# Keeping the split weights of the first half of the tokens in DRAM for the second half

## The chip, the core and the metric

The kernel runs on one core of a Trainium2 chip. The metric is device microseconds from the start to the end of one execution. Five engines work side by side, each through its own list of instructions, strictly in the order of that list: TensorE (PE; its weight loads are listed as PEld), VectorE (DVE), ScalarE (ACT), GpSimd (POOL) and SyncE (SP). They wait for each other through semaphores. DMAs are issued by SP and POOL here and carried out by 16 DMA engines.

## The reference, cut to what matters

One decoder layer, for 1024 prompt tokens and 8 decode tokens, all in float32:

```
h    = rmsnorm(x) ; proj = h @ w_in                # w_in: 1024 x 2304 = 18 tiles of 128 columns
pool = pooling mixer of proj[:, :512]              # tiles 0 to 3
rwkv = RWKV-7 mixer of proj[:, 512:]               # tiles 4 to 17, a recurrence over the tokens
x    = x + concat(pool, rwkv) @ w_out
x    = x + relu(rmsnorm(x) @ w_up)^2 @ w_down ; y = rmsnorm(x)
```

## The kernel before, in words

A float32 product is made of three fast ones. A weight `W` is split into `h` (W rounded to the format that TensorE takes at full rate, float32r) and `l = W - h`; the tokens likewise. `gemm` (L177) adds up h·h, h·l and l·h. So each weight costs, beside its load, one rounding copy on ACT and one subtraction on DVE.

`weights(src)` (L155) does this in pieces of 128 x 512 (256 KB): POOL loads the piece into a buffer `wr` (4 of them), ACT writes `wh`, DVE writes `wl` (6 buffers each). One column tile of `w_in` is two pieces. A piece can be split only when TensorE has finished with the piece six before it.

The input projection goes twice through all 18 tiles of `w_in`, because the tokens go in two halves: `project` (L272) and `pool_group` (L731) are called with `half` 0 and 1, and each time call `weights` for the tile. For a tile, TensorE does two token blocks of 24 matmuls of 256 columns, written into `pj`. Tiles are taken in the order 16, 17 (low rank inputs, `z`), 8, 4, 12 (k, r, v of the first head pair), 9, 5, 13, then the pool tiles 0 to 3, then 10, 6, 14, 11, 7, 15. A string, `ORDER` (L40), names the steps; within it a scheduler puts every instruction into its engine's list when the kernel is built, by its own estimate of when the inputs are there. So a change in one place can move instructions on every engine.

Around the projections, `stage1` (L346) prepares the recurrence for a head pair (it ends in `bv`, the matmul `pb`, and the matmuls `sc` and `bkt`), `inverse` (L474) inverts small triangular blocks through DRAM, and `chain` (L569) runs the recurrence (`pcs`, `py`) with short dependent steps on TensorE, ACT and DVE, whose result `ys` POOL stores to a scratch tensor `mix`. TensorE fills the time between chain steps with projections. `later_tokens` (L818) brings in the tokens of the second half; their raw tiles `xr` use the `wr` buffers too. The output projection (`mx`) and the MLP (`up`, `dn`) follow.

Of the kernel before, what the change touches and what calls it, by code (L numbers as in the profile page):

```python
# [8 lines left out]
F32R = mybir.dt.float32r  # L9
# [6 lines left out]
P = 128  # L16
D = 1024
# [19 lines left out]
NWH = 6  # L37
# [50 lines left out]
def build(nc, tc, I, O, dbg=None):  # L88
    with ExitStack() as ctx:
        _build(ctx, nc, tc, I, O, dbg or {})  # L90


def _build(ctx, nc, tc, I, O, dbg):
    V, A, PE, SY, GP = nc.vector, nc.scalar, nc.tensor, nc.sync, nc.gpsimd

    def f32(ap):
        return ap.bitcast(F32)

    def act(out, in_, func=AF.Copy, bias=0.0, scale=1.0, **k):
        A.activation(out, in_, func, bias=bias, scale=scale, **k)  # L100

    def open_pool(stack, name, bufs=1, **k):
        return stack.enter_context(tc.tile_pool(name=name, bufs=bufs, **k))
# [6 lines left out]
    wp = open_pool(ctx, "weights")  # L110
    ps_d = open_pool(ctx, "psd", 2, space=PSUM)
    ps_m = open_pool(ctx, "psm", 2, space=PSUM)
    dr = open_pool(ctx, "scratch", space=DRAM)
# [38 lines left out]
        act(out, out, AF.Exp, scale=-1.0, bias=last_bias)  # L152


    def weights(src, into=None):  # L155

        out = []
        n = int(np.prod(src.shape[1:]))
        for o in range(0, n, 512):
            w = min(512, n - o)  # L160
            raw = wp.tile([P, 512], F32, tag="wr", name="wr", bufs=NWR)
            if len(src.shape) > 2:
                GP.dma_start(raw.rearrange("p (m c) -> p m c", c=P), src)
            else:
                GP.dma_start(raw[:, :w], src[:, o:o + w])
            if into:
                h, l = into
            else:
                h = wp.tile([P, 512], F32R, tag="wh", name="wh", bufs=NWH)
                l = wp.tile([P, 512], F32R, tag="wl", name="wl", bufs=NWH)  # L170
            with tc.high_priority(offset=LEADW):
                act(h[:, :w], raw[:, :w])
                V.tensor_tensor(l[:, :w], raw[:, :w], f32(h[:, :w]), op=ALU.subtract)  # L173
            out += [(h[:, c:c + P], l[:, c:c + P]) for c in range(0, w, P)]
        return out

    def gemm(ps, w, ops):  # L177
# [84 lines left out]
    def project_block(m, w, b, use):  # L262
        n = SEG[b][1]
        first = m == 17 and b < 2
        ps = (ps_y if first else ps_d).tile([P, 512], F32, tag="y" if first else "d", name=f"pj{m}_{b}")
        gemm(ps[:, :n], w, [(X[b][0][:, k, :n], X[b][1][:, k, :n]) for k in range(KT)])
        with tc.high_priority(offset=LEADE):
            use(b, n, ps, X[b][2])

    ahead, late = {}, {}  # L270

    def project(m, half, use):  # L272
        w = ahead.pop(m, None) or weights(I["w_in"][m])
        for b in (2 * half, 2 * half + 1):
            if b in late:
                with tc.high_priority(offset=LEADX):
                    next(late.pop(b))
            project_block(m, w, b, use)
# [6 lines left out]
    def shifted(j, half, out):  # L285

        mu = col(V_MU, j)

        def use(b, n, ps, rs):
            l0 = 256 * (b % 2)  # L290
            pr = s1.tile([P, 264], F32, tag="pr", name=f"pr{j}_{b}", bufs=3)
            V.tensor_tensor(pr[:, :n], ps[:, :n], rs[:, :n], op=ALU.mult)
            act(out[:, l0:l0 + n], pr[:, :n], scale=omu[:, j:j + 1])
            d = out[:, l0 + 1:l0 + 256]
            V.scalar_tensor_tensor(d, pr[:, 0:255], mu, d, ALU.mult, ALU.add)
            if b:
                d = out[:, l0:l0 + 1]
                V.scalar_tensor_tensor(d, carry[:, j:j + 1], mu, d, ALU.mult, ALU.add)
            if b < 3:
                act(carry[:, j:j + 1], pr[:, 255:256])  # L300
            else:
                d = out[:, l0 + 256:l0 + 264]
                V.scalar_tensor_tensor(d, prevT[:, j, :], mu, d, ALU.mult, ALU.add)
                act(tailS[:, j, :], pr[:, 255:264])

        project(4 + j, half, use)
# [424 lines left out]
    def pool_group(g, half):  # L731
        win = 2 << g
        u, d = big(f"u{g}_{half}", f"u{g % 2}"), big(f"d{g}_{half}", f"d{g % 2}")
        e = d if g == 0 else big(f"e{g}_{half}", "e")
        if half:
            act(u[:, 0:16], ucar[:, g, :])
        else:
            GP.memset(u[:, 0:16], 0.0)

        def use(b, n, ps, rs):  # L740
            l0 = 16 + 256 * (b % 2)
            V.tensor_tensor(u[:, l0:l0 + n], ps[:, :n], rs[:, :n], op=ALU.mult)

        w = weights(I["w_in"][g])
        for i in range(2):
            project_block(g, w, 2 * half + i, use)
            yield
        n = HALF[half][1]
        pw_sb = pp.tile([P, P], F32, tag="pw", name=f"pw{g}_{half}")
        GP.dma_start(pw_sb, I["pool_w"][g])  # L750
        if half:
            act(tailU[:, g, :], u[:, 16 + 497:16 + 520])
        else:
            act(ucar[:, g, :], u[:, 512:528])
        src, w, i, o = u, 1, g % 2, 1
        while w < win:
            dst = (d, e)[i]
            V.tensor_tensor(dst[:, o:528], src[:, o:528], src[:, o - w:528 - w], op=ALU.add)
            src, w, i = dst, 2 * w, 1 - i
            o += w  # L760
        c = 16
        if half:
            V.tensor_tensor(poold[:, g, :], poold[:, g, :], u[:, 528:536], op=ALU.add)
            V.scalar_tensor_tensor(d[:, 528:536], poold[:, g, :], 1.0 / win, u[:, 528:536], ALU.mult, ALU.subtract)
        else:
            V.tensor_tensor(d[:, 16:32], d[:, 16:32], cst[:, C_RC + 16 * g:C_RC + 16 * g + 16], op=ALU.mult)
            V.tensor_tensor(d[:, 16:32], d[:, 16:32], u[:, 16:32], op=ALU.subtract)
            c = 32
        V.scalar_tensor_tensor(d[:, c:528], d[:, c:528], 1.0 / win, u[:, c:528], ALU.mult, ALU.subtract)
        yield  # L770
        for o, w in ((0, 256), (256, n - 256)):
            ps = ps_m.tile([P, 512], F32, tag="m", name=f"po{g}_{half}_{o}")
            PE.matmul(ps[:, :w], pw_sb, d[:, 16 + o:16 + o + w], start=True, stop=True)
            act(d[:, 16 + o:16 + o + w], ps[:, :w], scale=col(V_PS, g))
        QM.dma_start(mix_d[g][half], d[:, 16:16 + n])
# [3 lines left out]
    def pools(half, part):  # L779

        if part == 0:
            groups[half] = [pool_group(g, half) for g in range(4)]
        for g in ((0, 1, 0, 1, 0, 1), (2, 3, 2, 3, 0, 1, 2, 3), (2, 3))[part]:
            next(groups[half][g], None)
# [6 lines left out]
    units = [Unit(n % 4, n // 4) for n in range(8)]  # L791

    starts = [token_block(b) for b in range(2)]
    ahead[16] = weights(I["w_in"][16, :, 0:512])
    next(starts[0])
    ahead[16] += weights(I["w_in"][16, :, 512:])
    for t in starts:
        next(t)
    ahead[17] = weights(I["w_in"][17])
    SY.dma_start(cst, I["consts"])  # L800
    for t in starts:
        next(t)
# [15 lines left out]
    def later_tokens():  # L818
        with tc.high_priority(offset=LEADX):
            late.update((b, token_block(b)) for b in (2, 3))  # L820
            next(late[2])
            ahead[16] = weights(I["w_in"][16])
            next(late[3])

    st_d = ExitStack()
# [9 lines left out]
    for c in ORDER.split():  # L835
        if c[0] in calls:
            call, of = calls[c[0]]
            call(of[int(c[1])])
        elif c[0] == "P":
            pools(int(c[1]), int(c[2]))  # L840
        else:
            {"Q": pool_rows, "T": later_tokens, "L": lambda: low_rank(1), "D": decode_start}[c]()
# [14 lines left out]
    def x1s(m, c, n):  # L857

        h = int(c >= 512)
        return x1[h][:, m, c - 512 * h:c - 512 * h + n]  # L860
# [74 lines left out]
    with tc.tile_pool(name="opb", bufs=1, reuse_waits="tile") as op:  # L935
        ops = [mixed(op, k, 1, 3) for k in range(KT - 1)]
        for m in range(KT):
            w = weights(I["w_out"][m, :, :(KT - 1) * P])
# [12 lines left out]
    w = weights(I["w_up"][0])  # L951
# [20 lines left out]
    for g in range(7):  # L972
        ups_of(4 * g + 4)
        for m in range(KT):
            w = weights(I["w_down"][g, m])
# [20 lines left out]
    for b, (c, n) in enumerate(BLK):  # L996
        ss = ps_u.tile([P, 512], F32, tag="u", name=f"ss3{b}")
        acc = tmp(f"acc3{c}", "acc")[:, :n]
        for m in range(KT):
            down(7, m, b, ws[m])  # L1000
            d = x1s(m, c, n)
# [85 lines left out]
```

## Time and profile before

| | |
|---|---|
| median of 3 runs | 1378.54 us (1377.88 to 1382.42) |
| the profiled execution | 1379.3 us, its span 1377.5 us |
| TensorE busy | 1304.7 us, 95% of the span |
| VectorE busy | 809.3 us, 59% |
| ScalarE busy | 567.7 us, 41% |
| first half of the projection | about 9 to 194 us |
| second half | about 200 to 440 us |
| output projection and MLP | from about 470 us on |

The span runs from the first to the last instruction; the execution's own time is 1.8 us longer. From about 600 us on TensorE is never idle for long, and nothing there is touched by the change. A time written in brackets behind an instruction in the rows below is what its engine sat idle before it, and the arrow names what ended the wait.

### The profile page before, as it was taken

To read this page: it belongs to the slowest core of one execution; us is meant where nothing else is said; L and a number is where in the kernel's file an instruction comes from. 1 tells how busy PE (TensorE), PEld (TensorE's weight loads), DVE (VectorE), ACT (ScalarE), POOL (GpSimd) and SP (SyncE) were. 2 spreads that over 40 slices of the span, in tenths; PEclk is the share of its full clock that TensorE was granted. 3 is DMA by queue.
4 is the path that set the end of the run, shared out by engine and by line. 5 is a ranking of instruction groups with operands and counts; after the bars stand their busy time and mean duration, and the time that the engine had idled before them with its cause. 6 is when DMAs were issued, how large, how long until landed. Compare 5 with 4: busy or idle time off the path is not lost.

```text
span 1377.5 us, 24283 instructions
## 1 busy us (share of the span) xinstructions
PE 1304.7 (95%) x9748; PEld 1149.1 (83%) x9748; DVE 809.3 (59%) x1824; ACT 567.7 (41%) x1310; POOL 152.1 (11%) x301
## 2 busy tenths in 40 slices
PE   6999987999999899899999999999999999999996
PEld 6988776888877577699898999999999999999986
DVE  7887667748976754648644534435445354453447
ACT  7656775766766667626311211112112121121123
POOL 3112001101101100111000010100101000001000
PEclk9999997999999889989999999999999999999998
DMA  7234123311321542522111111111111111111103
GB/s 217 69 86 117 38 62 80 86 52 55 78 63 34 153 131 68 191 69 72 51 47 46 47 47 46 48 45 47 54 39 54 47 39 54 40 49 51 47 9 123
DMA packets 75312, 94.79 MB, mean 69 GB/s; under 512 B 46168, under 2 KB 52440, under 8 KB 75192
## 3 DMA queue, kind: packets, MB, share of 16 engines
q0 software_dynamic: 20480, 66.04, 15.4%
q1 hardware_dynamic: 53392, 25.36, 7.0%
q8 instruction: 76, 1.25, 0.4%
q10 hardware_dynamic: 1328, 1.85, 0.4%
q14 instruction: 36, 0.29, 0.1%
HBM read 79.67 MB, written 13.78 MB: 68 GB/s over the span
## 4 chain that ended last, share of the span: by engine, by line
PE 78%; ACT 9%; DVE 7%; issue 3%; DMA 3%; POOL 0%; SPq 0%; DVEq 0%; ACTq 0%; POOLq 0%
PE dn L183 26%; PE up L183 26%; PE pj L183 7%; PE mx L183 6%; PE sc L414 2%; ACT SV L100 1%; PE pcs L598 1%; PE pcs L592 1%; ACT Es L100 1%; DMA mr<-mix 1%; PE py L588 1%; ACT ys L100 1%; DVE wl L173 1%; DMA wr<-in_w_in 1%; DVE tm L515 1%
## 5 line engine op out<-in xcount | busy, mean ns | idle before, releaser
L100 ACT ACTIVATE wh<-wr 128x512 fp32r<-128x512 f32 x230 | 143.1, 626 | 359.6 <-PE dn L183 276.3
L183 PE MATMUL up<-h2h,wl 128*128 128x260 f32 (+1 forms) x768 | 245.6, 320 | 0.0
L183 PE MATMUL up<-h2h,wh 128*128 128x260 f32 (+1 forms) x768 | 245.0, 320 | 0.5 <-DVE u L929 0.5
L183 PE MATMUL up<-h2l,wh 128*128 128x260 f32 (+1 forms) x768 | 244.9, 319 | 0.0
L183 PE MATMUL dn<-uh,wl 128*128 128x512 f32 (+1 forms) x720 | 231.0, 321 | 0.0
L183 PE MATMUL dn<-ul,wh 128*128 128x512 f32 (+1 forms) x720 | 230.6, 320 | 0.0
L183 PE MATMUL dn<-uh,wh 128*128 128x512 f32 (+1 forms) x720 | 230.3, 320 | 0.0
L968 DVE TENSOR_TENSOR x<-dn,x 128x260 f32<-128x260 f32 (+1 forms) x192 | 99.0, 516 | 189.4 <-PE dn L183 189.4
L173 DVE TENSOR_TENSOR wl<-wr,wh 128x512 fp32r<-128x512 f32 x230 | 156.2, 683 | 55.3 <-ACT wh L100 51.9
L183 PE MATMUL pj<-xh,wh 128*128 128x256 f32 (+1 forms) x576 | 173.1, 301 | 12.6 <-ACT wh L100 9.5
L183 PE MATMUL pj<-xh,wl 128*128 128x256 f32 (+1 forms) x576 | 170.4, 296 | 0.0
L183 PE MATMUL pj<-xl,wh 128*128 128x256 f32 (+1 forms) x576 | 170.0, 295 | 0.0
L183 PEld LDWEIGHTS up<-h2l,wh 128*128 128x128 f32 x768 | 144.4, 188 | 12.2 <-DVE h2l L911 0.4
L183 PEld LDWEIGHTS up<-h2h,wh 128*128 128x128 f32 x768 | 144.2, 188 | 11.7 <-DVE u L929 0.9
L183 PEld LDWEIGHTS up<-h2h,wl 128*128 128x128 f32 x768 | 144.4, 188 | 11.1
L100 ACT ACTIVATE uh<-u 128x260 fp32r<-128x260 f32 (+1 forms) x96 | 47.2, 492 | 238.5 <-DVE u L930 238.5
L183 PEld LDWEIGHTS dn<-ul,wh 128*128 128x128 f32 x720 | 135.5, 188 | 10.9 <-issue 0.2
L183 PEld LDWEIGHTS dn<-uh,wh 128*128 128x128 f32 x720 | 135.7, 188 | 10.5
L183 PEld LDWEIGHTS dn<-uh,wl 128*128 128x128 f32 x720 | 135.4, 188 | 10.6 <-issue 0.2
L183 PEld LDWEIGHTS pj<-xh,wh 128*128 128x128 f32 x576 | 111.3, 193 | 18.3 <-ACT wh L100 9.5
L929 DVE SCALAR_TENSOR_TENSOR u<-up,rs 128x260 f32<-128x260 f32 (+1 forms) x96 | 49.5, 516 | 121.0 <-PE up L183 114.3
L183 PEld LDWEIGHTS pj<-xl,wh 128*128 128x128 f32 x576 | 111.3, 193 | 4.2 <-issue 3.3
(293 smaller groups left out, 2117.4 us busy)
## 6 DMA issues: line engine op xcount, KB each, us to landing
wr<-in_w_in POOLq DMA_DIRECT2D x72, 256.0 KB, 3.1
wr<-in_w_up POOLq DMA_DIRECT2D x64, 256.0 KB, 2.9
wr<-in_w_down POOLq DMA_DIRECT2D x64, 256.0 KB, 2.9
wr<-in_w_out POOLq DMA_DIRECT2D x26, 256.0 KB, 3.2
xr<-in_xT SPq DMA_DIRECT2D x16, 256.0 KB, 3.7
mr<-mix SPq DMA_DIRECT2D x8, 260.0 KB, 4.1
x<-in_xT SPq DMA_DIRECT2D x2, 1040.0 KB, 8.1
blk<-AA SPq DMA_DIRECT2D x16, 128.0 KB, 2.6
```

The lines of the kernel that those rows point to most:

```text
L100: A.activation(out, in_, func, bias=bias, scale=scale, **k)
L173: V.tensor_tensor(l[:, :w], raw[:, :w], f32(h[:, :w]), op=ALU.subtract)
L183: PE.matmul(ps, lhs, rhs, start=i == 0, stop=i == n - 1)
L414: PE.matmul(scs[h][:, c, :], BK[R[h], c, :, :], AR[R[h], c, :, h, :], start=True, stop=True)
L515: V.tensor_tensor(pr[:, q], l[:, q].unsqueeze(2).to_broadcast([64, m, m, m]), r[:, q].rearrange("p k j -> p j k").unsqueeze(1).to_broadcas ...
L588: PE.matmul(py[u][:, c, :, :], SV[:, c, u], B.AR[u][:, c, 1, :, :], start=True, stop=False)
L592: PE.matmul(pa[:, u], TT[:, 4 * u + c, :, :], Q[:, u], start=True, stop=True)
L598: PE.matmul(pu[:, u], B.BKT[u][:, c, :, :], SV[:, c, u], start=True, stop=True)
L929: V.scalar_tensor_tensor(u, ps[:, :n], 0.0, rs2[:, cs], ALU.max, ALU.mult)
L968: V.tensor_tensor(d, ps[:, :n], d, op=ALU.add)
```

## The change

In the first half each piece, once split, is also stored to DRAM: `wh` and `wl` go to `win_d[m]`, two stores of 256 KB per piece, issued by POOL. In the second half `weights_in` (new) takes a tile from there: POOL loads `wh` and `wl` straight into their buffers, and the load of the raw weight, the copy on ACT and the subtraction on DVE of that piece are gone.

```diff
-    def weights(src, into=None):
+    def weights(src, into=None, keep=None):
...
                 act(h[:, :w], raw[:, :w])
                 V.tensor_tensor(l[:, :w], raw[:, :w], f32(h[:, :w]), op=ALU.subtract)
+            if keep:
+                for d, t in zip(keep, (h, l)):
+                    GP.dma_start(d[:, o:o + w], t[:, :w])
             out += [(h[:, c:c + P], l[:, c:c + P]) for c in range(0, w, P)]
         return out
+
+    win_d = [[dr.tile([P, D], F32R, name=f"win{x}{m}") for x in "hl"] for m in range(18)]
+
+    def weights_in(m, half):
+
+        if half == 0:
+            return weights(I["w_in"][m], keep=win_d[m])
+        out = []
+        for o in (0, 512):
+            h, l = (wp.tile([P, 512], F32R, tag=x, name=f"{x}{m}", bufs=NWH) for x in ("wh", "wl"))
+            for d, t in zip(win_d[m], (h, l)):
+                GP.dma_start(t, d[:, o:o + 512])
+            out += [(h[:, c:c + P], l[:, c:c + P]) for c in range(0, 512, P)]
+        return out
...
     def project(m, half, use):
-        w = ahead.pop(m, None) or weights(I["w_in"][m])
+        w = ahead.pop(m, None) or weights_in(m, half)
...
-        w = weights(I["w_in"][g])
+        w = weights_in(g, half)
...
-    ahead[16] = weights(I["w_in"][16, :, 0:512])
+    ahead[16] = weights(I["w_in"][16, :, 0:512], keep=[d[:, 0:512] for d in win_d[16]])
...
-            ahead[16] = weights(I["w_in"][16])
+            ahead[16] = weights_in(16, 1)
```

The scheduler places all lists anew. Three places matter below. The first is ACT at the start of the first half, behind the statistics of the first token blocks (`ms`, `tt`, `rs`). Before, the copies of tile 8 and the tiles after it (`wh<-wr`) stand among the steps of the low rank inputs (`z`):

```order
L100 ACTIVATE wh<-wr 128x512
L100 ACTIVATE tt_277<-ms_276 128x256
L100 ACTIVATE wh<-wr 128x512
L100 ACTIVATE z_318<-pr_0_347,ona 128x256
L100 ACTIVATE carry<-pr_0_347 128x1
L100 ACTIVATE rs_209<-tt_277 128x256
L100 ACTIVATE wh<-wr 128x512 x4
L100 ACTIVATE z_318<-pr_1_377,ona 128x256
```

In the changed kernel no copy stands there; the first one comes behind three exponentials and logarithms of `z`, twelve rows further on:

```order
L100 ACTIVATE z_365<-pr_1_482,ona 128x256
L100 ACTIVATE carry<-pr_1_421 128x1
L100 ACTIVATE z_362<-z_362 64x512
L100 ACTIVATE za_364<-z_362 64x512
L100 ACTIVATE carry<-pr_1_482 128x1
L100 ACTIVATE z_362<-z_362 64x512
L100 ACTIVATE z_365<-z_365 128x512
L100 ACTIVATE z_362<-z_362 64x512
L100 ACTIVATE wh<-wr 128x512
L100 ACTIVATE z_365<-z_365 128x512
L100 ACTIVATE zw_363<-z_362 64x512
```

The copies have moved down; the order of the other rows is the same.

The second place is POOL in the same stretch. Before, its list is loads of raw pieces, with two small clears between:

```order
L165 DMA wr<-in_w_in 128x512 x4
L738 MEMSET u_0_1123 128x16
L738 MEMSET u_0_1164 128x16
L165 DMA wr<-in_w_in 128x512 x19
L738 MEMSET u_0_1469 128x16
```

In the changed kernel the stores of the pieces stand between the loads (`winh_115`, `winl_116` are tile 8, 107 and 108 tile 4, 123 and 124 tile 12):

```order
L165 DMA wr<-in_w_in 128x512 x4
L755 MEMSET u_0_1191 128x16
L755 MEMSET u_0_1236 128x16
L176 DMA winh_115<-wh 128x512
L176 DMA winl_116<-wl 128x512
L165 DMA wr<-in_w_in 128x512
L176 DMA winh_115<-wh 128x512
L176 DMA winl_116<-wl 128x512
L176 DMA winh_107<-wh 128x512
L176 DMA winl_108<-wl 128x512
```

A load now stands behind stores, each of which waits for the split of its piece.

The third place is TensorE near the end of the second half, where `stage1` of the last head pair but one reaches its matmul `pb_1`. Before, all projections (`pj`) are over at this row:

```order
L587 MATMUL pcs<-SV_3_4091,AR_137 128x128
L587 MATMUL pcs<-SV_3_4091,AR_139 128x128
L588 MATMUL py_3_1_4962<-AR_139,SV_3_4091 128x128
L383 MATMUL pb_1_5210<-bv_1_5208,cst 128x512
L592 MATMUL pcs<-Q_3_3_5031,TT_160 128x128 x2
L414 MATMUL sc_2_0_5224<-AR_137,BK 128x128 x3
```

In the changed kernel projections stand on both sides of it; 28 of the 1728 come behind it:

```order
L200 MATMUL pj_3_5969<-xl_2673,wh_5901 128x264
L400 MATMUL pb_1_5262<-bv_1_5260,cst 128x512
L605 MATMUL py_3_0_5013<-AR_173,SV_3_4167 128x128
L604 MATMUL pcs<-SV_3_4167,AR_173 128x128
L604 MATMUL pcs<-SV_3_4167,AR_175 128x128
L605 MATMUL py_3_1_5014<-AR_175,SV_3_4167 128x128
L200 MATMUL pj_3_5969<-xh_2672,wl_5902 128x264
L200 MATMUL pj_3_5969<-xh_2672,wh_5901 128x264
```

The steps of `stage1` and of the chain have moved up against the projections.

## Rows read from the trace of the kernel before

**Rows 1.** The page's first lines: span, busy time of TensorE.

```profile
span 1377.5 us, 24283 instructions
PE 1304.7 (95%) x9748; PEld 1149.1 (83%) x9748; DVE 809.3 (59%) x1824; ACT 567.7 (41%) x1310; POOL 152.1 (11%) x301
```

**Rows 2.** Stretches: length, then busy us of each engine, granted clock, DMA share, GB/s.

```profile
40.00:60.00 20.00, 20.00 (x149) 17.94 (x148) 17.20 (x37) 14.57 (x33) 3.76 (x7) 1.00 0.32 104
190.00:400.00 210.00, 187.94 (x1788) 162.46 (x1787) 155.14 (x415) 146.15 (x362) 25.42 (x50) 0.94 0.27 75
440.00:475.00 35.00, 26.58 (x119) 19.05 (x120) 27.44 (x74) 22.39 (x60) 5.92 (x11) 0.85 0.50 137
```

**Rows 3.** The page's groups of the split on ACT and DVE, all weights.

```profile
L100 ACT ACTIVATE wh<-wr 128x512 fp32r<-128x512 f32 x230 | 143.1, 626 | 359.6 <-PE dn L183 276.3
L173 DVE TENSOR_TENSOR wl<-wr,wh 128x512 fp32r<-128x512 f32 x230 | 156.2, 683 | 55.3 <-ACT wh L100 51.9
```

**Rows 4.** DMA issues (count, KB each, median us to landing), POOL's queue, POOL's issue instruction.

```profile
wr<-in_w_in POOLq DMA_DIRECT2D x72, 256.0 KB, 3.1
mr<-mix SPq DMA_DIRECT2D x8, 256.0 KB, 4.8
mix<-d POOLq DMA_DIRECT2D x4, 256.0 KB, 3.0
q0 software_dynamic: 20480, 66.04, 15.4%
L165 POOL DMA_DIRECT2D wr<-in_w_in x72 | 39.0, 542 | 235.0 <-DVE wl L173 131.1 <-ACT AA L100 32.6 <-ACT r L100 10.7
```

**Rows 5.** ACT in order of time, start of the first half: start us, us.

```profile
24.77 0.62 ACT L100 ACTIVATE wh<-wr 128x512 fp32r<-128x512 f32 x1
29.50 0.63 ACT L100 ACTIVATE wh<-wr 128x512 fp32r<-128x512 f32 x1 [1.44 <-DMA wr<-in_w_in]
34.34 0.49 ACT L100 ACTIVATE k<-pr,ona 128x256 f32<-128x256 f32 x1
35.23 1.66 ACT L100 ACTIVATE z<-z 64x512 f32<-64x512 f32 x3
```

**Rows 6.** TensorE in order of time, same stretch; tiles 17, 8 and 4.

```profile
25.26 0.28 PE L183 MATMUL pj<-xh,wl 128*128 128x256 f32 x1
26.01 0.36 PE L183 MATMUL pj<-xh,wh 128*128 128x256 f32 x1 [0.47 <-DVE pr L292]
33.58 0.36 PE L183 MATMUL pj<-xh,wh 128*128 128x256 f32 x1 [0.30 <-ACT z L100]
```

**Rows 7.** The chain that ended last, from 33.58 us: 96 matmuls in 11.57 us.

```profile
33.58 11.57 PE pj L183 x96
```

**Rows 8.** POOL in order of time: loads of tile 8, start of the first half.

```profile
16.77 1.14 POOL L165 DMA_DIRECT2D wr<-in_w_in  x2 [9.44 <-DVE wl L173]
```

**Rows 9.** TensorE in order of time between the halves.

```profile
198.17 1.13 PE L372 MATMUL pk<-t,cst 128*128 128x512 f32 x2 [2.94 <-ACT w L100]
209.33 1.66 PE L247 MATMUL ss<-acc,cst 128*128 128x256 f32 x4 [4.78 <-DVE acc L231]
215.75 2.08 PE L383 MATMUL pb<-bv,cst 128*128 128x512 f32 x2 [4.76 <-DVE bv L381]
```

**Rows 10.** A stretch behind the first of these waits, columns as in rows 2.

```profile
200.00:202.00 2.00, 2.00 (x10) 1.91 (x9) 1.02 (x3) 1.93 (x6) 0.54 (x1) 0.50 0.75 206
```

**Rows 11.** DVE between the halves: first and last of six `wl` ahead of `bv`.

```profile
196.21 0.69 DVE L173 TENSOR_TENSOR wl<-wr,wh 128x512 fp32r<-128x512 f32 x1
214.35 0.68 DVE L173 TENSOR_TENSOR wl<-wr,wh 128x512 fp32r<-128x512 f32 x1
214.95 0.74 DVE L381 SCALAR_TENSOR_TENSOR bv<-r,vec,k 128x512 f32<-128x512 f32 x1
```

**Rows 12.** SP's queue between the halves: five loads of raw tokens.

```profile
159.22 40.58 SPq L221 DMA_DIRECT2D xr<-in_xT  x5
```

More of the change, by code (lines that the diff above doesn't have):

```diff
@@ L793, in _build @@
     starts = [token_block(b) for b in range(2)]
-    ahead[16] = weights(I["w_in"][16, :, 0:512])
+    ahead[16] = weights(I["w_in"][16, :, 0:512], keep=[d[:, 0:512] for d in win_d[16]])
     next(starts[0])
-    ahead[16] += weights(I["w_in"][16, :, 512:])
+    ahead[16] += weights(I["w_in"][16, :, 512:], keep=[d[:, 512:] for d in win_d[16]])
     for t in starts:
         next(t)
-    ahead[17] = weights(I["w_in"][17])
+    ahead[17] = weights_in(17, 0)
     SY.dma_start(cst, I["consts"])
```

## The prediction

> **What bounds the kernel.** Start with the page's first lines. TensorE is busy 1304.7 of 1377.5 us [rows 1], so the change cannot win much more than the 73 us in which it is idle, plus what a lowered clock costs it. VectorE and ScalarE have slack over the span, so the work that the change takes from them is worth only as much TensorE time as was waiting for it. Read next the table by stretches. Early in the first half TensorE is busy throughout: 20.00 us of 20 from 40 to 60 us [rows 2]. There nothing can be won, and every delay of a weight is paid in full. From 190 to 400 us TensorE is idle 210 - 187.9 = 22.1 us, from 440 to 475 us 35 - 26.6 = 8.4 us [rows 2]: what can be won lies here. Then the list of TensorE in order of time says who is late. Between the halves three waits stand, 2.9, 4.8 and 4.8 us, the last for `bv` on VectorE [rows 9].
>
> **What is removed.** 36 copies on ACT of 0.626 us and 36 subtractions on DVE of 0.683 us [rows 3], 22.5 and 24.6 us in the second half, and 36 raw loads. Three places of TensorE's time are touched.
>
> Between the halves, six subtractions stand ahead of `bv` on DVE, the first at 196.21 and the last at 214.35 us, directly before `bv` at 214.95 [rows 11]. DVE works without a pause for most of that time, and consecutive ones start 0.6 us apart (214.35 to 214.95), so six are worth 3.6 us. The raw tokens also come sooner, since the weights of the second half no longer use the `wr` buffers for which SP's five loads queue for 40.6 us [rows 12]. Against that, ACT still has to wait for the last raw tokens ahead of the sigmoids of `stage1`, which it now does in a single run. From below I take nothing, from above the waits for `acc` and `bv` together, 4.8 + 4.8 = 9.5 us [rows 9]; the value is 3 us, near the DVE rows.
>
> At the end of the second half, 28 projection matmuls now stand behind `pb_1`. At 11.57 / 96 = 0.12 us [rows 7] they are 3.4 us of work for a stretch with 8.4 us of idle time [rows 2]. The clock granted there was 0.85, and with fewer pauses some of that comes back. Bounds 0 and 8.4 us; I take 4.
>
> In the rest of the second half the idle time is 22.1 less the three waits (12.5), so 9.6 us in many small pieces, mostly latencies of chain steps that a shorter list does not cut. Bounds 0 and 5 us; I take 1.5. Gains together: 8.5 us.
>
> **What is added.** 72 stores and 36 more loads of 256 KB; the weights of the second half take four loads per tile where there were two. POOL's issue of one is 0.542 us, landing 3.0 to 4.8 us for the nearest rows [rows 4]. In the second half this is covered: a tile's buffers come free three tiles ahead, that is at least two tiles or 2 x 48 x 0.12 = 11.5 us before its first matmul, and four issues and a landing take 4 x 0.54 + 4.8 = 7.0 us. If that cover were gone, each tile would cost up to 7 us; the nearest row in POOL's list that could hold loads up, a store of `ys`, stands where it has finished some 100 matmuls before the tile is wanted.
>
> In the first half the price lies in the order of ACT's list, not in the bytes. Tile 8 was loaded by 20 us (issued at 16.77 [rows 8], and 3.1 us to land). Its first copy ran at 24.77 [rows 5], and TensorE, done with tile 17 at 25.26, went on with tile 8 at 26.01 and with tile 4 at 33.58 [rows 6]. In the changed list that copy comes behind three steps of `z` that ended at 35.23 + 1.66 = 36.9 us before. Ahead of them stood seven copies, each worth some 0.53 us of ACT's time, two waits for raw loads (1.44 and 0.37), and three steps of `k` (34.34 to 35.23) [rows 5]: 3.7 + 1.8 + 0.9 = 6.4 us, which no longer stand there. If ACT alone set the pace, the copy would start at 30.5; but `z` passes back and forth between ACT and DVE, and following each step gives 32.3, so that `wl` is there at about 33.5. TensorE then idles some 8 us where it idled under 2. Tile 8 takes 48 x 0.12 = 5.8 us, and its first dozen matmuls run slower: behind the wait between the halves TensorE did 10 matmuls in 2 us at a granted clock of 0.50, the 1.2 GHz level [rows 10], 0.2 us each in place of 0.12. This adds 1 to 2.5 us. So tile 4 starts at about 33.5 + 5.8 + 1.8 = 41.1, 7.5 us later than before. Low bound: the copy at 30.5, no change of clock, 31.8 + 5.8 - 33.6 = 4.0 us. High bound: the `z` steps end where they did, `wl` is there at 38.2, 38.2 + 5.8 + 2.3 - 33.6 = 12.7 us. Nothing in the next 60 us absorbs this, as TensorE is full there [rows 2].
>
> Everything behind on POOL is late too: a load waits for the stores ahead of it, and these for the split. What the next load finds is three tiles of split weights, 17 us of TensorE's work, against stores, load and landing of some 6 us. I take 1 us for what slips through, with bounds of 0 and 3, because the landing can grow from 3.1 towards 4.8 us [rows 4] while stores and loads share the DMA engines. POOL's queue moved 66.04 MB in 15.4% of the span [rows 4], 311 GB/s while busy, or 0.84 us for 256 KB. A tile's two loads and four stores are 5.1 us of all engines, against 5.8 us of TensorE per tile: just enough.
>
> **Sum.** + 7.5 + 1 - 3 - 4 - 1.5 = 0.0 us, against the profiled execution's 1379.3 us, which is 0.8 us above the median of the runs. I forecast 1379 us: no change that can be told, which is within 0.3% or 4.1 us.
>
> **The rivals.** *Faster.* The waits of the second half belong to ACT and DVE more than I grant: 6 us between the halves, 6 at the end, 3 in the rest, and the stall at the start is 5 us: 1379.3 - 10 = 1369. For it: DVE is busy 155 of 210 us in that stretch [rows 2], and 24.6 us less is a sixth. Against it: most waits there are short steps that depend on each other.
>
> *Slower at the start.* The stall goes to 10 us or more and the second half gives back 2: 1379.3 + 8 to 9, about 1388. The place is ACT's copy behind `z`; it decides from a stall of 12.6 us if the gains are as I took them, or of 8.6 if only half of them come. For it: the delay is certain in its order and only its size is open, while each gain has nothing as its low bound.
>
> *Slower by the transfers.* A store or load of the split format takes longer on the DMA engines than the plain 0.84 us. No row shows such a transfer, so the price is a bound: if each takes twice as long, a tile of the first half needs 2 x 0.84 + 4 x 1.68 = 8.4 us, 2.6 more than TensorE's 5.8, over the eight tiles that stand back to back (8 to 1): 21 us, so 1400. It decides from 1.03 us a store, at which the engines no longer keep up. Against it: stores of float32 of that size land as fast as loads, 3.0 and 3.1 us [rows 4]. The Trainium skill, "DMA: Bandwidth & Descriptors", section "SWDGE vs HWDGE vs iDMA", says that a DMA into a float32r destination always counts as a cast, and that only GpSimd issues such DMAs; it gives no price, and no run here shows one. By that rule all 144 new transfers would be of this kind, and the rival would be the place to look first.
>
> **How the numbers follow.** No change 0.40, faster 0.27, slower at the start 0.21, by the transfers 0.12. So slower is 0.33. The forecast's own range is 1375 to 1383; to leave out no more than 2 in 10 it must reach to the faster rival at 1369 and past the first slower one at 1388, so 1368 to 1392.
>
> **What would show it.** The new trace should have TensorE idle for 6 to 9 us around 26 to 34 us, ended by `wh` or `wl`; tile 4 starting near 41 us; a granted clock below 1 behind it; from there to 190 us the same busy share as before; `pb` between the halves waiting 1 to 3 us less; 440 to 475 us (moved by the shift so far) with 4 to 5 us idle. No wait of TensorE for a load of `winh` or `winl` should stand in the second half. It is wrong if that wait shows, if landings in the first half rise above 6 us, if the stall at the start is under 4 or over 12 us, or if the second half shortens by more than 12 us.

## The result, and the profile after

The changed kernel takes 1390.63 us (median of 7 runs, 1387.04 to 1399.75) against 1377.88 before (7 runs): a ratio of 1.0095, 95% interval 1.0075 to 1.0116. It is slower, by some 13 us in the medians. The profiled execution took 1389.3 us. Its page begins so:

```profile
span 1387.4 us, 24384 instructions
PE 1303.7 (94%) x9748; PEld 1148.7 (83%) x9748; DVE 793.2 (57%) x1788; ACT 549.6 (40%) x1274; POOL 209.7 (15%) x409
```

Against [rows 1], the busy time of DVE and ACT fell by 16 and 18 us, that of POOL rose by 58 us, and TensorE's is the same within 1 us. So the 9.9 us by which the span grew are, on balance, time in which TensorE waits; the profiled executions show 9.9 of the 12.8 us between the medians. To find where, both executions are cut at the same four events of TensorE: the first matmul of tile 4, of tile 15 in the first half, of tile 17 in the second half, and the first `up`. Columns as in [rows 2]. Before:

```profile
0.00:33.58 33.58, 22.51 (x152) 21.31 (x153) 26.70 (x80) 23.95 (x52) 11.44 (x33) 1.00 0.72 218
33.58:186.84 153.26, 146.99 (x1397) 128.80 (x1397) 115.36 (x290) 103.23 (x249) 18.62 (x39) 1.00 0.25 71
186.84:235.13 48.29, 33.08 (x176) 27.43 (x175) 37.34 (x95) 30.96 (x72) 6.45 (x12) 0.75 0.34 95
235.13:629.40 394.27, 366.25 (x3363) 307.14 (x3362) 258.66 (x653) 251.47 (x645) 50.52 (x96) 0.95 0.30 89
629.40:1377.50 748.10, 735.89 (x4668) 664.46 (x4666) 371.27 (x710) 158.03 (x294) 65.03 (x121) 1.00 0.16 49
```

After:

```profile
0.00:40.33 40.33, 22.91 (x153) 22.07 (x153) 30.10 (x85) 27.68 (x60) 18.73 (x47) 0.92 0.80 254
40.33:200.08 159.75, 149.71 (x1403) 131.50 (x1401) 114.23 (x286) 99.30 (x241) 53.65 (x105) 0.99 0.60 176
200.08:246.41 46.33, 31.69 (x172) 26.33 (x171) 33.02 (x86) 27.92 (x66) 7.00 (x13) 0.78 0.43 117
246.41:639.60 393.19, 363.50 (x3363) 304.32 (x3362) 244.29 (x623) 236.66 (x615) 65.25 (x124) 0.95 0.38 108
639.60:1387.40 747.80, 735.89 (x4668) 664.47 (x4666) 371.60 (x710) 158.06 (x294) 65.03 (x121) 1.00 0.15 49
```

The differences of the lengths are the account of the change, and they can be set beside the terms of the sum:

| stretch | before, us | after, us | difference | predicted |
|---|---|---|---|---|
| to tile 4 | 33.58 | 40.33 | +6.75 | +7.5 |
| rest of the first half | 153.26 | 159.75 | +6.49 | +1 |
| between the halves | 48.29 | 46.33 | -1.96 | -3 |
| second half, output projection | 394.27 | 393.19 | -1.08 | -5.5 |
| MLP | 748.10 | 747.80 | -0.30 | 0 |
| sum | 1377.50 | 1387.40 | +9.90 | 0.0 |

So the start stall is there almost as forecast, and two terms are far off: the rest of the first half loses 6.5 us, and the second half gives back hardly anything. The rows of each follow.

The start, TensorE in order of time (last matmul of tile 17, first of tiles 8 and 4, answering to [rows 6]):

```profile
24.99 0.28 PE L200 MATMUL pj<-xh,wl 128*128 128x256 f32 x1
32.67 0.58 PE L200 MATMUL pj<-xh,wh 128*128 128x256 f32 x1 [7.40 <-ACT wh L100]
...
40.33 0.28 PE L200 MATMUL pj<-xh,wh 128*128 128x256 f32 x1
```

ACT in order of time, at the start and near 69 us (answering to [rows 5]):

```profile
30.45 1.65 ACT L100 ACTIVATE z<-z 64x512 f32<-64x512 f32 x3
32.00 0.61 ACT L100 ACTIVATE wh<-wr 128x512 fp32r<-128x512 f32 x1
...
69.24 1.28 ACT L100 ACTIVATE wh<-wr 128x512 fp32r<-128x512 f32 x2 [4.28 <-issue]
70.43 0.49 ACT L100 ACTIVATE r<-pr,ona 128x256 f32<-128x256 f32 x1
70.82 0.36 ACT L100 ACTIVATE AA<-sc 64x256 f32<-64x256 f32 x1
```

The copy of tile 8 runs at 32.00 us (the prediction followed the list to 32.3), behind the `z` steps, and TensorE waits 7.40 us for it. Later the same picture comes back in small. At 69.24 ACT has sat idle for 4.28 us in front of a copy, and `r` and `AA`, which are behind it in ACT's list, are late. DVE waits for `r`; `AR`, which is behind that step in DVE's list, is late in turn, and TensorE waits for it. DVE and TensorE in order of time:

```profile
70.95 0.49 DVE L312 SCALAR_TENSOR_TENSOR r<-pr,vec,r 128x255 f32<-128x255 f32 x1 [2.54 <-ACT r L100]
...
72.49 0.63 PE L443 MATMUL bkt<-cst,BK 128*128 128x128 f32 x4 [1.99 <-DVE AR L438]
```

The page gives no releaser for ACT's 4.28 us ("issue"). POOL's list in order of time shows the likely one: three raw loads issued from 63.13 us on, directly behind stores that waited for splits.

```profile
18.60 1.10 POOL L165 DMA_DIRECT2D wr<-in_w_in  x2
...
62.09 0.53 POOL L176 DMA_DIRECT2D winl<-wl  x1 [0.48 <-DVE wl L173]
62.61 0.53 POOL L176 DMA_DIRECT2D winh<-wh  x1
63.13 1.64 POOL L165 DMA_DIRECT2D wr<-in_w_in  x3
```

These three took 6.1 us to land (median of the stretch from 63 to 65 us), so they landed from 69 us on; tile 8's, issued at 18.60, took 6.7.

TensorE's wait at 72.49 stands for only a part of the 6.49 us. Cut at the first matmuls of tiles, the loss is 2.3 us from tile 4 to tile 0, where the wait is; 1.3 from tile 0 to tile 10; 1.8 from tile 10 to tile 6, where TensorE waits 2.2 us for a small load of the pool tiles (`pw`), as it did before (2.0 us), but the granted clock of the stretch is 0.84 where it was 1.00; 0.1 from tile 6 to tile 11; and 1.0 from tile 11 to tile 7. The parts behind tile 0 were not followed to a cause.

The page's DMA issues and POOL's queue (answering to [rows 4]) have the bytes and the landing of a raw load over the whole program:

```profile
q0 software_dynamic: 38336, 94.36, 22.1%
...
wr<-in_w_in POOLq DMA_DIRECT2D x36, 256.0 KB, 4.9
```

A raw load lands after 4.9 us where it took 3.1. The queue's bytes grew by 94.36 - 66.04 = 28.32 MB and its time by 22.1% of 1387.4 less 15.4% of 1377.5 = 94.5 us, which for the 108 transfers more (144 new ones, 36 raw loads gone) is 300 GB/s or 0.87 us for 256 KB, against 0.84 before: a transfer of the split format costs the DMA engines nearly what a plain one does.

Between the halves, TensorE in order of time (answering to [rows 9]):

```profile
210.39 1.64 PE L264 MATMUL ss<-acc,cst 128*128 128x256 f32 x4 [2.98 <-DVE acc L248]
217.88 1.12 PE L389 MATMUL pk<-t,cst 128*128 128x512 f32 x2 [1.95 <-ACT w L100]
220.11 1.13 PE L264 MATMUL ss<-acc,cst 128*128 128x256 f32 x4 [1.11 <-DVE acc L248]
227.11 2.05 PE L400 MATMUL pb<-bv,cst 128*128 128x512 f32 x2 [5.86 <-DVE bv L398]
```

They sum to 11.9 us, against 12.5 in [rows 9]. The splits are gone from DVE there, and `bv` is waited for longer, not shorter. The chain of work in this stretch says what is ahead of it (only the rows that carry the point):

```profile
203.10 2.12 ACT xh L100 x5
...
207.10 5.12 DMA xr<-in_xT
212.24 0.91 ACT xh L100 x2
...
226.21 0.76 DVE bv L398
```

From 203.10 us, when TensorE has finished the first half and frees the `xh` buffers, a single line of steps runs over the raw tokens, their last load, the copies, the sums and `stage1` to `bv`. No split of a weight is on it. Before, the chain of the same stretch had four subtractions:

```profile
190.93 2.12 ACT xh L100 x5
...
196.29 0.60 DVE wl L173
...
210.45 0.15 DVE wl L173
...
211.73 0.60 DVE wl L173
...
214.43 0.60 DVE wl L173
```

They are 1.95 us of the chain. From the `xh` copies to `pb` it took 215.75 - 190.93 = 24.8 us before and 227.11 - 203.10 = 24.0 after, so the gain there is 0.8 us; another 1.1 of the 1.96 us lie ahead of 203.10, where TensorE is busy throughout in both.

### The profile page after: what moved, and what is told of

It reads as the page before. It is cut to its first block, busy times and chain, and to the rows that moved or that the text cites. A ratio compares the mean times of both kernels' runs of the same rounds, so it can differ in the third digit from the quotient of the medians.

```text
span 1387.4 us, 24384 instructions
## 1 busy us (share of the span) xinstructions
PE 1303.7 (94%) x9748; PEld 1148.7 (83%) x9748; DVE 793.2 (57%) x1788; ACT 549.6 (40%) x1274; POOL 209.7 (15%) x409
## 3 DMA queue, kind: packets, MB, share of 16 engines
q0 software_dynamic: 38336, 94.36, 22.1%
## 4 chain that ended last, share of the span: by engine, by line
PE 77%; ACT 7%; DVE 7%; issue 4%; DMA 3%; POOL 1%; DVEq 0%; SPq 0%; POOLq 0%; ACTq 0%
PE dn L200 26%; PE up L200 26%; PE pj L200 8%; PE mx L200 5%; PE sc L431 2%; PE pcs L609 1%; PE pcs L615 1%; DVE tm L532 1%; ACT SV L100 1%; DMA wr<-in_w_in 1%; DMA mr<-mix 1%; PE py L605 1%; ACT Es L100 1%; PE py L631 1%; ACT TT L100 1%
## 5 line engine op out<-in xcount | busy, mean ns | idle before, releaser
L100 ACT ACTIVATE wh<-wr 128x512 fp32r<-128x512 f32 x194 | 121.0, 626 | 358.0 <-PE dn L200 276.2
L200 PE MATMUL pj<-xl,wh 128*128 128x256 f32 (+1 forms) x576 | 173.7, 302 | 0.0
L173 DVE TENSOR_TENSOR wl<-wr,wh 128x512 fp32r<-128x512 f32 x194 | 132.0, 684 | 48.7 <-ACT wh L100 44.9
L200 PEld LDWEIGHTS dn<-ul,wh 128*128 128x128 f32 x720 | 135.5, 188 | 10.9 <-issue 0.2
L200 PEld LDWEIGHTS pj<-xh,wh 128*128 128x128 f32 x576 | 113.0, 196 | 22.1 <-ACT wh L100 17.3
```

What stands on the lines that cost most here:

```text
L200: PE.matmul(ps, lhs, rhs, start=i == 0, stop=i == n - 1)
```

## The experiments

All times are medians; each ratio is to runs of the kernel before on the same chip, with its 95% interval. Eleven kernels were run. The theory of the prediction says: a stall at the start by the order of ACT's list, little else. Its rivals by now: the transfers as such cost the time, wherever they are issued; and, for the second half, that the loads cost what the splits did.

**Stores alone** (the second half splits again):

```diff
     def weights_in(m, half):
+        if half == 1:
+            return weights(I["w_in"][m])
```

> Here the first half stores as in the changed kernel (same lists on every engine), but the second half splits every weight again and never loads what was stored. If the loss lies in the first half (the start stall of 7 us, and 6.5 us more by the time tile 15 of the second count begins at 200 us), tile 16 of the second half starts at 211 to 214 us as after the change, and the time is before + 12 to 16, 1390 to 1394 us: the loads of the second half are then worth 0 to 4 us. If the second half's loads do the harm instead, this kernel is back at 1378 to 1382.

1390.3 us, ratio 1.0084 (1.0066 to 1.0101); tile 16 of the second half starts at 213.63 us. The whole loss stands in the first half, and the loads of the second half change nothing that can be told.

**Loads alone** (no stores; the second half loads `w_in` into `wh` and `wl`):

```diff
-            if keep:
-                for d, t in zip(keep, (h, l)):
-                    GP.dma_start(d[:, o:o + w], t[:, :w])
...
-            for d, t in zip(win_d[m], (h, l)):
-                GP.dma_start(t, d[:, o:o + 512])
+            for t in (h, l):
+                GP.dma_start(t, I["w_in"][m][:, o:o + 512])
```

> Nothing is stored; the second half loads two pieces for each raw one, straight from w_in into wh and wl (so wl holds the weight itself in place of the rest, and the result is not the layer's). If the loss lies in the stores and in the lists around them, the start is as before (tile 4 at 33.6 us, second half from 200 us), and the time is 1373 to 1378 us, what the second half saves by itself. If more transfers in the second half or the moved stage steps cost as much as the saved splits, it is 1378 to 1383.

1378.7 us, ratio 1.0000 (0.9988 to 1.0012), in the range that was written for "costs as much as the saved splits". The first half is as before (tile 4 at 33.24, tile 15 at 186.50).

**The first four tiles not kept**:

```diff
+FRESH = (16, 17, 8, 4)
...
     def weights_in(m, half):
+        if m in FRESH:
+            return weights(I["w_in"][m])
...
```

> The first four tiles (16, 17, 8, 4) are not stored and are split again in the second half; the other 14 are stored and loaded. ACT's copies of tile 8 then stand ahead of the steps of z, as before the change. If the start stall is a matter of that order, tile 4 starts at 33 to 35 us and the time falls by 6 to 8 us from the changed kernel, to 1382 to 1385; the loss after tile 13 stays. If the transfers as such cost the time, only 16 of 72 stores are gone and the time is 1386 to 1390.

1378.4 us, ratio 0.9999 (0.9984 to 1.0015): better than either theory had it. Both losses of the first half are gone but for 1.7 us (tile 4 at 33.81, tile 15 at 188.50), with 56 of the 72 stores still made. TensorE's first matmuls of tiles 8 and 4, and the stretch behind them, columns as in [rows 2]:

```profile
26.04 0.36 PE L203 MATMUL pj<-xh,wh 128*128 128x256 f32 x1 [0.42 <-DVE pr L312]
...
33.81 0.36 PE L203 MATMUL pj<-xh,wh 128*128 128x256 f32 x1 [0.49 <-ACT z L101]
```
```profile
33.00:68.00 35.00, 34.29 (x259) 31.20 (x258) 30.14 (x70) 24.92 (x60) 15.77 (x29) 1.00 0.76 234
```

The DMA engines are 0.76 busy from 33 to 68 us (0.24 in the same window before, 0.91 in the changed kernel), raw loads issued there land in 4.7 us, and TensorE is idle for 0.7 us of 35. Busy DMA engines and late landings, at that level, do not by themselves cost the first half its time.

**Stores issued by SP**, as plain float32:

```diff
-    win_d = [[dr.tile([P, D], F32R, name=f"win{x}{m}") for x in "hl"] for m in range(18)]
+    win_d = [[dr.tile([P, D], F32, name=f"win{x}{m}") for x in "hl"] for m in range(18)]
...
-                    GP.dma_start(d[:, o:o + w], t[:, :w])
+                    SY.dma_start(d[:, o:o + w], f32(t[:, :w]))
```

> All 72 stores are kept with all their bytes, but SP issues them (as plain float32), so that no load on POOL stands behind a store, and ACT's first copies stand ahead of z again. If the order of the lists on POOL and ACT makes the loss, it is gone with it: 1374 to 1380 us, with landings of the raw loads perhaps still over 4 us. If the DMA engines are the cause (0.91 busy from 33 to 68 us after the change, 0.32 before), the loss of the first half stays but for the 7 us at the start: 1382 to 1387. A new wait may come on SP, where its other transfers (raw tokens, the inverse's blocks) would stand behind stores.

1391.5 us, ratio 1.0089 (1.0068 to 1.0111): no better, and worse than both theories had it. The start is nearly mended (tile 8 at 27.23, tile 4 at 35.63), and then it is lost elsewhere. ACT and TensorE in order of time:

```profile
45.69 0.63 ACT L100 ACTIVATE wh<-wr 128x512 fp32r<-128x512 f32 x1 [2.31 <-issue]
48.19 0.63 ACT L100 ACTIVATE wh<-wr 128x512 fp32r<-128x512 f32 x1 [1.78 <-PE pw L349]
51.72 0.67 ACT L100 ACTIVATE w<-pw,ona 128x512 f32<-128x512 f32 x1
...
52.45 1.22 PE L389 MATMUL pk<-t,cst 128*128 128x512 f32 x1 [3.15 <-ACT w L100]
```

Copies that wait stand ahead of `w` on ACT, and TensorE waits for `w`. The raw loads issued at 40.11 and 41.88 us landed 5.5 and 6.2 us later, just ahead of these two copies, so it is loads that they waited for, whatever the rows put the waits down to. The median landing of raw loads is 5.4 us here, with no store in POOL's list at all. So a landing grows by sharing the DMA engines; being queued behind stores on POOL is not needed for it. (The 0.32 that the expectation gives for before is the share from 40 to 60 us; from 33 to 68 us it was 0.24.)

**Tiles 16 and 17 not kept** (`FRESH = (16, 17)`):

> Only the first two tiles (16 and 17) are not stored and are split again in the second half. ACT's copies of tile 8 then stand ahead of z; the stores of tiles 8 and 4 remain, and tile 12's loads stand behind them. If the start stall hangs on the stores of 16 and 17, tile 4 starts at 33 to 35 us. Then: if the 6.5 us lost later in the first half follow from the late start, they go too and the time is 1378 to 1381; if they belong to loads that stand behind stores, they stay, and it is 1383 to 1386.

1385.5 us, ratio 1.0050 (1.0032 to 1.0068), in the range for loads that stand behind stores. **Tiles 8 and 4 not kept** (`FRESH = (8, 4)`):

> The counterpart: tiles 16 and 17 are stored, 8 and 4 are not. ACT's copies of tile 8 still stand behind the steps of z, as in the changed kernel. If the order on ACT makes the stall, tile 4 starts at 39 to 41 us. If the loss after it follows from the late start, the time stays at 1388 to 1391; if that loss comes from the stores of tiles 8 and 4 ahead of tile 12's loads, it is 1383 to 1385.

1387.6 us, ratio 1.0071 (1.0050 to 1.0093), between the two ranges. The start stall hangs on 16 and 17: with their stores left out tile 4 starts at 33.20 us, with those of 8 and 4 left out at 40.29, behind the same wait of 7.41 us for `wh`. The later loss does not simply follow from a late start. The first of the two kernels had no stall at the start and lost time between tiles 13 and 0. Its profiled execution is the slowest of its twelve (1396.4 us), so it shows the mechanism and not the usual size. Stretches, tile 13's first matmul to tile 0's and the middle of it, in that kernel; and, last, the same tiles with all four left out:

```profile
60.67:81.02 20.35, 18.02 (x86) 15.72 (x85) 11.04 (x28) 6.77 (x16) 4.96 (x10) 0.66 0.36 109
64.00:70.00 6.00, 4.26 (x19) 4.06 (x20) 5.67 (x17) 2.75 (x7) 1.08 (x2) 0.57 0.42 131
```
```profile
61.55:73.69 12.14, 12.04 (x86) 10.26 (x85) 11.49 (x28) 6.04 (x15) 2.88 (x6) 1.00 0.27 84
```

The same 86 matmuls take 20.35 us against 12.14. A wait of 2.33 us for `AR` at 65.74 is most of the idle time; the rest of the 8.2 us is the granted clock, 0.66 over the stretch where it was 1.00.

**The split by priority** (all stores kept):

```diff
+LEADK = 600
...
-            with tc.high_priority(offset=LEADW):
+            with tc.high_priority(offset=LEADK if keep else LEADW):
```

> All stores stay, but the copy and the subtraction of a stored tile get a higher priority when the lists are made, so that ACT copies tile 8 ahead of z again (tile 4 still behind it). If the order on ACT makes the stall, tile 8 starts at 26 to 28 us and tile 4 loses 1 to 3 us, and the time is 1380 to 1386. If it is tile 8's load that comes too late behind the stores of 16 and 17 (issued 1.8 us later than before the change), tile 8 starts after 29 us and the time is over 1386.

1393.3 us, ratio 1.0101 (1.0088 to 1.0114), by the second reading. POOL, ACT and TensorE in order of time:

```profile
15.93 0.55 POOL L166 DMA_DIRECT2D wr<-in_w_in  x1 [1.22 <-DMA winh<-wh]
...
23.48 0.63 ACT L101 ACTIVATE wh<-wr 128x512 fp32r<-128x512 f32 x1 [3.45 <-DMA wr<-in_w_in]
...
31.65 0.39 PE L201 MATMUL pj<-xh,wh 128*128 128x256 f32 x1 [1.17 <-DVE pr L310]
```

With the copy ahead of everything ACT waits 3.45 us for the raw load, which landed 7.5 us after its issue, and the token statistics (`ms`, `rs`) behind the copy are late instead; TensorE then waits 3.1 us for `acc`, 1.2 for `pr` and, between tiles 8 and 4, 4.3 for `zw`. So putting the copy first does not mend the stall, because the load is late too. In the changed kernel tile 8's raw weight itself is there only at 18.60 + 6.7 = 25.3 us; before, it was at 16.77 + 4.4 = 21.2 (4.4 being the landing of these two loads).

**Short stores** (as stores alone, 64 of 512 columns in each):

```diff
-                    GP.dma_start(d[:, o:o + w], t[:, :w])
+                    GP.dma_start(d[:, o:o + 64], t[:, :64])
```

> As the kernel that stores only (1390.3 us), but each store moves 64 of the 512 columns, an eighth of the bytes (so what stands in DRAM is not the weight; nobody reads it). The lists begin alike, with ACT's copies of tile 8 behind z. If the bytes on the DMA engines make the loss after the start, the landings fall to 3 us and the second half starts at 206 to 208 us: 1383 to 1386. If the lists make it, nothing much changes: 1387 to 1391. The start stall stays at 5 to 7.5 us by either.

1386.8 us, ratio 1.0057 (1.0042 to 1.0072), against 1390.3 with whole stores: between the two ranges. The start stall is the same (7.41 us, tile 4 at 40.26), although tile 8's loads, issued at 18.29, land after 3.0 us, at 21.3 as before the change. So the order of the lists makes that stall even when the load is there in time. Tile 16 of the second half starts at 208.34 us, 5.3 earlier, and from tile 4 to tile 15 the first half takes 154.6 us, against 160.0 with whole stores and 153.3 before. Landings from 33 to 140 us, whole stores and then short ones:

```profile
wr<-in_w_in POOLq DMA_DIRECT2D x28, 256.0 KB, 5.4
```
```profile
wr<-in_w_in POOLq DMA_DIRECT2D x28, 256.0 KB, 3.4
```

The bytes make the landings, and with them goes most of the loss after the start in these executions. The lists of the two kernels begin alike but are not the same row by row further on, so what the bytes alone cost there is not shown.

**No weights in the second half** (two resident tiles in place of all of them, and no stores):

```diff
-            for d, t in zip(win_d[m], (h, l)):
-                GP.dma_start(t, d[:, o:o + 512])
-            out += [(h[:, c:c + P], l[:, c:c + P]) for c in range(0, 512, P)]
-        return out
+        return [(wup[:, c:c + P], aup[:, c:c + P]) for c in range(0, 512, P)] * 2
...
```

> Nothing is stored, and in the second half nothing is loaded or split either: its 36 projections multiply with two weight tiles that are in SBUF from the start (so the result is not the layer's). The first half's lists are those of before. This is the most that the second half can give back. If its waits belong to the weights (the prediction took 8.5 us in all), the time falls to 1368 to 1372 us. If they belong to the tokens' loads between the halves and to the steps of stage1 and chain, the time stays at 1375 to 1380 and the waits for acc, w and bv between the halves stay near 12 us.

1368.4 us, ratio 0.9933 (0.9916 to 0.9951): 10.4 us less, where the prediction had granted 8.5 to the removed work. Between the halves the waits for `acc` and `bv` stay (2.7, 1.7 and 6.5 us), as the second reading had it; the gain comes behind them, in the 394 us up to `up`, which shrink to 382.6. So the second half does wait for its weights, if not between the halves.

**The first eight tiles not kept** (`FRESH = (16, 17, 8, 4, 12, 9, 5, 13)`):

> The first eight tiles are not stored and are split again; ten tiles, from the pool tiles on (73 us), are stored and loaded. If only the stores of the first four tiles cost time, this is the same as with those four left out, 1376 to 1380 us. If the stores between tile 12 and tile 13 cost something that the second half's loads gave back there, it is below 1376.

1375.5 us, ratio 0.9994 (0.9974 to 1.0015): the same as before. The median lies just under 1376, where the second reading begins, but the twelve runs spread from 1373.0 to 1387.6, so the two readings are not told apart. No version here that computes the layer beats the kernel before by more than its interval.

**Short loads** (as loads alone, 128 of 512 columns in each, used four times):

```diff
-                GP.dma_start(t, I["w_in"][m][:, o:o + 512])
+                GP.dma_start(t[:, :P], I["w_in"][m][:, o:o + P])
...
-            out += [(h[:, c:c + P], l[:, c:c + P]) for c in range(0, 512, P)]
+            out += [(h[:, :P], l[:, :P])] * 4
```

> The kernel that only loads (1378.7 us), with the same lists on TensorE, VectorE, ScalarE and GpSimd row by row, but each of its 72 loads moves 128 of the 512 columns, a quarter of the bytes, and the projections use these columns four times (the result is not the layer's). If the bytes of the second half's loads take back what the missing splits gave, the time falls to 1369 to 1373 us, near the 1368.4 of the kernel without any weights in the second half, and the landings of the inverse's blocks (TX, 4.2 us) fall to 3 to 3.5. If the lists of the second half are the cause (the order in which the steps now stand, POOL's issues), it stays at 1376 to 1380.

1373.3 us, ratio 0.9947 (0.9934 to 0.9961). The lists of TensorE, VectorE, ScalarE and GpSimd are those of loads alone, row by row; only the bytes differ, and with them 1.0000 becomes 0.9947, some 7 us, at the edge of the range written for the bytes. (The two profiled executions are 2.7 us apart, so their traces hold only a part of it.) Landings from the second half's start of tile 8 to `up`: loads alone, then short loads.

```profile
wl<-in_w_in POOLq DMA_DIRECT2D x28, 256.0 KB, 3.5
TX<-inv SPq DMA_DIRECT2D x6, 256.0 KB, 4.2
```
```profile
wl<-in_w_in POOLq DMA_DIRECT2D x26, 64.0 KB, 2.2
TX<-inv SPq DMA_DIRECT2D x6, 256.0 KB, 3.5
```

`TX`, which the inverse waits for, landed in 3.0 us before the change. TensorE waits 1.8 us for it with whole loads (1.6 in the changed kernel), and neither with short ones nor before. The raw tokens between the halves, 3.7 us before, land in 4.3 with whole loads and 2.9 with short ones. The transfers that the chain of steps waits for are slowed by the weights' own.

## Why the prediction was right and wrong

The forecast was no change at 1379 us; the time is 1390.6, inside the stated 1368 to 1392, near its end, and slower beyond the interval of the runs. That it lies inside is owed to the width of the range, which was drawn to take in the rivals, and not to the mechanism. The rival that forecast 1388 came nearest in time: its gain of 2 us in the second half is nearer to the 3.3 us that the executions show than the forecast's 8.5, but it wanted a start stall of 10 us or more, and the stall came out under the forecast. The thresholds stated for that rival leave out the 1 us of the next term, and with half of the gains the sum is 4.1 + 4.25 = 8.4 us, not 8.6; less that 1 us it decides from 7.4.

**The start, +7.5.** Right: 6.75 us, the copy at 32.00 us, tile 4 at 40.33, the clock at half for the first matmuls behind the wait (0.50 from 33 to 36 us). The mechanism holds too: the short stores show the same stall with the load there in time, so the order makes it, "not the bytes". What the prediction did not see is that the load is late as well, at 25.3 us and not by 20 (before, it was 21.2: these two landed after 4.4 us, not 3.1), so that moving the copy ahead, as in the split by priority, only moves the wait. What mends it is leaving the stores of tiles 16 and 17 out.

**The rest of the first half, +1.** This step failed: 6.5 us, over its bound of 3. It set three tiles of split weights against "stores, load and landing of some 6 us" and the engines' 5.1 us of transfers per tile against TensorE's 5.8. Both are averages, and they want a POOL that issues each load in time. The trace shows landings of 4.9 us in the median and 6.1 and more where loads meet stores, and, what the step left out, that a copy that waits for its load stands in ACT's list ahead of steps of `stage1` that TensorE's next work hangs on (69.24 us above). That accounts for 2.3 of the 6.5 us; the short stores speak for the bytes in most of the rest, and part of it is a lower granted clock, but these were not separated. The buffers' lead protects the weights, not what is queued behind them on ACT. It is a matter of when: with the 56 stores of the other 14 tiles the time is that of before, and adding the stores of 8 and 4 alone, or of 16 and 17 alone, brings a loss of 7 to 9 us.

**Between the halves, -3.** The right sign, -2.0, not by the rule of six subtractions of 0.6 us: of the six only 1.95 us stood on the chain, the chain is shorter by 0.8, and `bv` is waited for 1.1 us longer than before. With no weights at all the waits there are still 10.9 us together. They belong to the tokens and to `stage1`.

**The second half, -4 and -1.5.** Wrong by a size, and by a term that was set to nothing. The gains were taken as 5.5; the removed work is worth more (10.4 us with no weights at all, over the whole second half). But the prediction's "In the second half this is covered" was looked at only for the weights' own arrival. No wait for `winh` or `winl` stands there, as was forecast; the price is paid by the other transfers. Loads of a quarter of the bytes, in the same lists, leave a gain of 0.5%, whole loads leave none. The 28 projections behind `pb_1` moved the idle time rather than fill it. Taken 11.3 us later, by which tile 17 of the second half is shifted, TensorE is idle for 35 - 28.2 = 6.8 us from 451.3 to 486.3 us instead of 8.4, and in the 35 us behind that for 2.7 instead of 1.0. Two new waits for `pw`, 4.4 us together, are among them; one of 3.1 us stands in the kernel without weights too, so such a wait does not need the loads. Which of the slowed transfers costs how much of the 7 us was not separated, nor was the rest, 1373.3 with short loads against 1368.4 with none.

**The transfers.** The rival's price was wrong (0.87 us, not 1.03 or more), and yet the bytes matter in both halves. The Trainium skill, "DMA: Bandwidth & Descriptors", section "SWDGE vs HWDGE vs iDMA", says that a DMA into a float32r destination counts as a cast. By that rule the stores that SP issued into plain float32 were none; with them, and with other lists, the time was 1391.5 against 1390.6, so nothing here speaks for a price of the cast itself. The Trainium skill, "DMA: Bandwidth & Descriptors", section "Queues, rings and completion order", says that each DMA engine takes the queues that have work in turn. The trace agrees as far as it shows: SP's `TX` lands after 3.0 us before and 4.4 after the change, which loads POOL's queue.

## What to carry to other kernels

Replacing computation by a reload was paid here in DMA bytes, and the payer need not be the thing that is reloaded: look at every transfer that a chain of short steps waits for, not only at the buffers' lead. Where a start-up has no lead (here the first four tiles), extra transfers can reorder the lists and hold up the first weights (6.75 us here, with a granted clock of 0.50 behind the wait); with the stores of these four tiles left out, those of the other 14 took no time that could be told. And a copy that may wait for its data should be looked up in its engine's list for what stands behind it, since that is what is late next.

## What the runs showed of the hardware

- A stretch of 20 us with one wait of TensorE of 2.33 us had a granted clock of 0.66 in one execution, and was 8.2 us longer than without; in the changed kernel's profiled execution a wait of 1.99 us at the same step left the stretch at 1.00 (14.4 us from tile 13 to tile 0). Later in the first half the stretch with a wait of 2.2 us for `pw` had 0.84, and 1.00 before the change with 2.0 us. That may be why the kernels with such waits scatter (1380.9 to 1396.4 us with tiles 16 and 17 left out); it was not tested apart.
- A 256 KB load that lands in 3.1 us in the median took 4.9 with twice its bytes of stores around it, 5.4 where SP issued the stores, and 6.7 at the start, where the DMA share was 1.14 from 10 to 20 us (before the change 4.4, at 1.06).
- SP's issue of a store shows 0.32 us where nothing stands in its way, POOL's 0.53.
